# Layer 1's modulation groups 1 and 2 made as side steps of the latents' MLP in layer 0, loaded through GpSimd's queue

## The chip, the cores and the metric

The kernel runs on one core of a Trainium2 chip. The metric is the device time of one execution in microseconds; lower is better. A core has TensorE (PE, with its weight loads as PEld), VectorE (DVE), ScalarE (ACT), GpSimd (POOL) and SyncE (SP), which here only issues DMAs.

## The reference, cut to what matters

Two layers of a mixer network work on 256 latent tokens and 256 context tokens of width 1024, and a second network of two layers follows. Each of the first two layers begins with a modulation: one vector per stream goes through a matrix of 1024 x 6144, and its six parts shift, scale and gate the layer.

```
for i in range(DEPTH):
    m_l = (jax.nn.silu(c) @ mod_w + mod_b)[:, None, :]
    m_c = jax.nn.silu(c_ctx) @ mod_w + mod_b
    sh1_l, sc1_l, g1_l, sh2_l, sc2_l, g2_l = jnp.split(m_l, 6, axis=-1)
    ...
    p_lat = _ada(x, norm1, sh1_l, sc1_l) @ w_in
    p_ctx = _ada(ctx, norm1, sh1_c, sc1_c) @ w_in
    ... mixer (even: attention and rwkv; odd: ssd and gla) -> o_l, o_c
    x = x + g1_l * (o_l.astype(x.dtype) @ w_out)
    x = x + g2_l * _sq_relu_mlp(_ada(x, norm2, sh2_l, sc2_l), mlp_w1, mlp_w2)
```

The modulation depends on `c` and `c_ctx` alone, so it can be made at any time before its parts are read. Shift and scale 1 are read by layer 1's first norms, gate 1 by its output product, the rest by its MLP.

## The kernel before

All is float32. A product splits each operand into a rounded part and a remainder (`hi`, `lo`; ACT makes `hi` on L45, DVE `lo` on L46) and is made of three matmuls (`mm3`, L231 to L233). Weights come as tiles `w` of 128x1024 (512 KB), four buffers in the pool `wpool`, loaded by SP's queue in program order (`Stream.raw`, L32). One product tile of 128x256 with eight blocks of weights takes one `w` tile and 24 matmuls.

A modulation matrix is made in three groups of columns (`mod_steps`). A group has 16 units; a unit is one `w` tile of 512 KB and four narrow matmuls (128 rows, 32 columns, 256 wide; each stands in the trace as two instructions, L162) that add up in one PSUM bank. Two units are a step, with a `yield` behind it. Behind the last step ACT copies the bank (L166), PE transposes it four times (L169), and DVE adds the bias into `mT` (L171). With a `ring` the units are loaded into a ring of its own, four buffers, by the named engine; without one they go through SP's queue and the four buffers of `wpool`.

The latents' MLP of layer 0 (the call of `mlp` in `layer1`) has four parts of 16 product tiles each, 64 in all, eight of the first product and eight of the second. Its list `side` is advanced at n = 2 and 6 of each eight, so 16 times: two empty steps, the tables of the second network's rotation, the eight steps of layer 1's group 0 (ring of four buffers, GpSimd's queue, PSUM tag `po`), and the context's norm, whose first two tiles come together with the tail of group 0.

Then layer 1 norms the latents, makes the input product's first columns, and starts two mixers. `gla` (linear attention with gates) is a long chain of small DVE, ACT, POOL and PE work; its first half is written out ahead of the conv loop. The conv loop makes eight product tiles (512 wide, the last two 256), runs a five tap convolution over each (L860, L862) and a silu (L1223, L1225). Groups 1 and 2 of layer 1's modulation are written out behind the first of them, in one piece, through SP's queue and `wpool`, PSUM tag `mm` (two banks, which the conv products use too). Behind the loop come the second half of `gla`, eight products for `z` and `gs`, and the mixer `ssd`.

The order on each engine is not that of the program: a planner simulates the program with costs of its own and puts on each engine the ready instruction of highest priority, the priority being the order in which it was written out. On the chip each engine then takes its instructions strictly in that order, and each queue its DMAs. A side step is thus an instruction that the planner may take earlier, when it holds the engine for idle.

Of the kernel before, what the change touches and what calls it, by code (L numbers as in the profile page):

```python
# [76 lines left out]
class Kern:  # L77
# [720 lines left out]

        return h, sm, step

    def mlp(self, l, mp, x, w, sm, h=None, done=None, side=(), tags=("mm", "mm")):

        side = iter(side)
        nc, parts = self.nc, MLP_PARTS[l]
        g2 = self.ada(self.mT[l], self.V(f"norm2_{l}"), 3, mp, f"g2_{l}")
        with self.tc.high_priority():
            f = sm.rstd()
            early, h = h, []
            steps = self.norm_steps(mp, mp, x, f, w, g2, self.mT[l][:, 24:32, :], "h")
            if not early:  # L810
                h.extend(steps)
        NF = 7 if early else 0
        st = Stream(self, self.a[f"mlp{l}"])
        b0 = 0
        m = 32 // parts
        for i in range(parts):
            u = []
            for n in range(m):
                if i == 0 and n >= NF:
                    h.extend(steps)  # L820
                ps = self.gemm(st, b0, early if i == 0 and n < NF else h, tag=tags[n % 2])
                b0 += 8
                if n % 4 == 2:
                    next(side, None)
                r = mp.tile([P, 256], F32, tag="hf", name="relu", bufs=2)
                if i == 0 and n < NF:
                    b = mp.tile([P, 1], F32, tag="bias", name="bias", bufs=2)
                    nc.vector.tensor_copy(b, ps[:, 256:257])
                    nc.vector.tensor_tensor(r, ps[:, 0:256], f, op=ALU.mult)
                    nc.scalar.activation(r, r, AF.Relu, bias=b)  # L830
                else:
                    nc.scalar.activation(r, ps, AF.Relu)
                nc.scalar.activation(r, r, AF.Square)  # L833
                u.append(self.split(mp, r, 256, f"u{n}_"))
                if i == 0 and n < NF:
                    h.extend(itertools.islice(steps, 1))
            if i == 0:
                h.extend(steps)
            for n in range(8):
                ps = self.gemm(st, b0, u)  # L840
                b0 += m
                nc.vector.scalar_tensor_tensor(x[n], ps, self.mT[l][:, 40 + n, w : w + 1], x[n], op0=ALU.mult, op1=ALU.add)
                if done and i == parts - 1:
                    done(x[n])
                if n % 4 == 2:
                    next(side, None)
        for _ in side:
            pass
# [297 lines left out]
    def layer1(self, xc, xl, sm, hm, HL):  # L1146

        tc, nc, a = self.tc, self.nc, self.a
        L1, H, G = ExitStack(), ExitStack(), ExitStack()
        pool = lambda n, st=L1, side="left": st.enter_context(tc.tile_pool(name=n, bufs=1, side=side))  # L1150
        rp, kvp = pool("cossin", self.ctx), pool("kvp", self.ctx)
        pl, hl, hc = pool("l1"), pool("h1l"), pool("h1c", H)
# [6 lines left out]
        h = []  # L1159

        def norm(p, x, sm, w):
            g1 = self.ada(mT, self.V("norm1_1"), 0, pl, f"g1_1{w}")
            with ExitStack() as M:
                xp = pool("x1", M)
                h.append([])
                for i in self.norm_steps(xp, p, x, sm.rstd() if sm else self.rms(xp, x), w, g1, mT[:, 0:8, :], "h"):
                    h[-1].append(i)
                    yield

        with ExitStack() as M:  # L1170
            self.gap(M, 64)
            mp = pool("mlp", M, "right")
            sm, sm2 = Sum(self), sm

            def side():
                yield
                yield
                with ExitStack() as R:
                    rope.extend(self.rope2(pool("rope", R), rp))
                yield  # L1180
                yield from self.mod_steps(1, 0, mp, "po", (mp, 4, nc.gpsimd))
                for i, _ in enumerate(norm(hc, xc, None, 1)):
                    if i % 2:
                        yield

            rope = []
            self.mlp(0, mp, xl, 0, sm2, hm, sm.add, side(), ("mm", "po"))
        HL.close()
        lg = pool("lg", G)
        up = self.load("gk_up", lg)  # L1190
# [11 lines left out]
        for kk in range(8):  # L1202
            w = st.cols(40 * 128 + 512 * kk, 512)
# [13 lines left out]
        cp = pool("cv", C, "right")  # L1217
        cw, cb = [self.small(self.V(n), ALU.mult, 0.5, tag=n, pool=cp) for n in ("conv_w", "conv_b")]

        def silu(t, last):  # L1220

            u = cp.tile([P, 512], F32, tag="th", name="th")[:, : t.shape[-1]]
            i = nc.scalar.activation(u, t, AF.Tanh)  # L1223
            self.issue(i, last)
            nc.vector.scalar_tensor_tensor(t, u, 1.0, t, op0=ALU.add, op1=ALU.mult)  # L1225
            return i

        tanh, mods = [], (x for i in (1, 2) for x in self.mod_steps(1, i, cp, "mm"))
        for i in range(8):
            t = (xs + bm + cm)[i]  # L1230
            self.conv(cp, self.gemm(st, 72 + 8 * i, *(h if i < 6 else h[1:])), i, t, cw, cb)
            if i == 0:
                for _ in mods:
                    pass
            tanh.append(silu(t, last))
        for _ in mods:
            pass
        self.table(tanh)
        for _ in gla:
            pass  # L1240
# [22 lines left out]
        with ExitStack() as B:  # L1263
# [4 lines left out]
            h, sm, step = self.mlp_enter(1, pool("mh1", HL, "right"), 0)  # L1268
# [566 lines left out]
```

## Time and profile before

| what | us |
|---|---|
| median of 3 runs (lowest, highest) | 2023.52 (2015.88, 2032.34) |
| the profiled execution | 2024.35 |
| its span in the trace | 2022.6 |
| PE busy in the span | 1894.8 (94%) |
| DVE busy | 1420.9 (70%) |
| ACT busy | 1160.8 (57%) |
| POOL busy | 285.5 (14%) |

What lies around the span is 1.75 us. Matmuls are pipelined and their ends are modelled, so PE busy is not PE at its peak. Times of day in this text are us from the start of the span.

### The profile page before, as it was taken

What the parts mean: (1) busy time and instruction counts of PE and PEld (TensorE: products, weight loads), DVE (VectorE), ACT (ScalarE), POOL (GpSimd) and SP (SyncE); (2) the same over time, 40 slices, a digit from 0 to 9 for tenths busy, and PEclk for the clock granted to TensorE, in tenths of its full rate; (3) what the DMA queues carried; (4) which work ended last, traced back from release to release, by engine and by line L of the source; (5) the groups of instructions that cost most, each with busy time, mean ns of one, the idle gap of its engine ahead of it and who ended that gap; (6) DMA issues with size and microseconds to landing.
All of it is one profiled execution on the core that took longest, in us unless ns stands there. A gap on an engine that the chain in (4) does not pass through costs nothing.

```text
span 2022.6 us, 42324 instructions
## 1 busy us (share of the span) xinstructions
PE 1894.8 (94%) x16330; PEld 1709.2 (85%) x16330; DVE 1420.9 (70%) x2962; ACT 1160.8 (57%) x2527; POOL 285.5 (14%) x423
## 2 busy tenths in 40 slices
PE   5999989889999999999979999999999999989997
PEld 2986668669889998999638779999889999879997
DVE  3775966589767685576678978567777666677664
ACT  3654653465646676565545758476565555465553
POOL 1421110230100000001230210000012211002210
PEclk8999989899999999999979999999999999999999
DMA  8542530635116676755366435666325554324553
GB/s 304 165 137 76 171 126 22 199 95 166 43 35 189 188 238 203 244 176 167 120 222 189 143 105 175 186 187 189 124 84 168 188 188 146 103 86 157 187 187 116
DMA packets 91785, 313.26 MB, mean 155 GB/s; under 512 B 10304, under 2 KB 17728, under 8 KB 91584
## 3 DMA queue, kind: packets, MB, share of 16 engines
q1 hardware_dynamic: 81072, 291.55, 44.9%
q10 hardware_dynamic: 8208, 10.63, 1.7%
q0 software_dynamic: 2304, 8.39, 1.2%
q8 instruction: 128, 2.10, 0.4%
q14 instruction: 73, 0.60, 0.1%
HBM read 309.48 MB, written 1.05 MB: 154 GB/s over the span
## 4 chain that ended last, share of the span: by engine, by line
PE 73%; DVE 12%; ACT 5%; DMA 5%; issue 3%; POOL 2%; POOLq 0%; ACTq 0%; SPq 0%; DVEq 0%
PE mm L232 15%; PE mm L233 15%; PE mm L231 15%; PE po L232 3%; PE po L231 3%; PE po L233 3%; DMA w<-in_mod 2%; DVE lo L46 2%; DMA w<-in_w_in 2%; PE sc L540 1%; PE mm L162 1%; PE po L1395 1%; ACT hi L45 1%; DMA m<-in_memT 1%; PE po L1458 1%
## 5 line engine op out<-in xcount | busy, mean ns | idle before, releaser
L46 DVE TENSOR_TENSOR lo<-w,hi 128x512 fp32r<-128x512 f32 x948 | 654.6, 696 | 259.2 <-ACT hi L45 240.5
L45 ACT CAST hi<-w 128x512 fp32r<-128x512 f32 x948 | 577.4, 618 | 408.0 <-PE mm L232 308.3
L231 PE MATMUL mm<-u_h,hi 128*128 128x256 f32 x1120 | 314.3, 281 | 0.0
L233 PE MATMUL mm<-u_h,lo 128*128 128x256 f32 x1120 | 314.1, 281 | 0.0
L232 PE MATMUL mm<-u_l,hi 128*128 128x256 f32 x1120 | 313.3, 280 | 0.1
L231 PEld LDWEIGHTS mm<-u_h,hi 128*128 128x128 f32 x1120 | 210.5, 188 | 2.2 <-ACT hi L45 1.2
L232 PEld LDWEIGHTS mm<-u_l,hi 128*128 128x128 f32 x1120 | 210.9, 188 | 0.3 <-DVE u_l L225 0.3
L233 PEld LDWEIGHTS mm<-u_h,lo 128*128 128x128 f32 x1120 | 210.8, 188 | 0.1
L162 PE MATMUL mm<-w,cs 128*32 128x256 f32 x640 | 68.9, 452 | 30.8 <-DMA w<-in_mod 30.5
L1600 POOL TENSOR_TENSOR ut<-ut,gt 128x256 f32<-128x256 f32 x44 | 54.4, 1237 | 193.0 <-ACT hi L45 164.6
L162 PEld LDWEIGHTS mm<-w,cs 128*32 128x32 f32 x640 | 18.6, 118 | 59.4 <-DMA w<-in_mod 35.2
L225 DVE TENSOR_TENSOR u_l<-relu,u_h 128x256 fp32r<-128x256 f32 x96 | 40.8, 426 | 30.0 <-ACT u_h L224 29.8
L355 POOL TENSOR_SCALAR sht<-shf,mu 128x256 f32<-128x256 f32 x28 | 37.6, 1341 | 110.1 <-ACT shf L353 110.1
L224 ACT CAST u_h<-ut 128x256 fp32r<-128x256 f32 x44 | 17.9, 407 | 59.0 <-POOL ut L1600 59.0
L225 DVE TENSOR_TENSOR u_l<-ut,u_h 128x256 fp32r<-128x256 f32 x44 | 18.7, 425 | 45.0 <-ACT u_h L224 45.0
L264 POOL TENSOR_SCALAR hf<-hf,g,mT 128x256 f32<-128x256 f32 x24 | 18.7, 779 | 211.3 <-ACT h1h L263 111.8
L231 PE MATMUL mm<-h0h,hi 128*128 128x256 f32 x130 | 39.8, 308 | 7.4 <-ACT shf L353 3.6
L1552 POOL TENSOR_TENSOR xl<-xl,yy 128x256 f32<-128x256 f32 x16 | 14.2, 889 | 225.5 <-DVE yy L1551 225.5
L69 POOL TENSOR_TENSOR sq<-sq 128x256 f32<-128x256 f32 x24 | 20.7, 863 | 153.5 <-ACT sq L61 150.5
L233 PE MATMUL mm<-h0h,lo 128*128 128x256 f32 x130 | 38.4, 295 | 3.1 <-DVE lo L46 3.1
L833 ACT ACTIVATE relu<-relu 128x256 f32<-128x256 f32 x96 | 39.7, 417 | 2.4
L224 ACT CAST u_h<-relu 128x256 fp32r<-128x256 f32 x96 | 38.6, 405 | 2.3
(1126 smaller groups left out, 6096.6 us busy)
## 6 DMA issues: line engine op xcount, KB each, us to landing
w<-in_mlp SPq DMA_DIRECT2D x192, 512.0 KB, 4.1
w<-in_w_in SPq DMA_DIRECT2D x102, 512.0 KB, 4.1
w<-in_ffn_in SPq DMA_DIRECT2D x88, 512.0 KB, 4.1
w<-in_mod SPq DMA_DIRECT2D x80, 512.0 KB, 5.2
w<-in_ffn_out SPq DMA_DIRECT2D x44, 512.0 KB, 4.6
w<-in_w_out SPq DMA_DIRECT2D x40, 512.0 KB, 4.5
w<-in_mod POOLq DMA_DIRECT2D x16, 512.0 KB, 8.0
w<-in_memkv SPq DMA_DIRECT2D x8, 512.0 KB, 4.0
```

The costliest lines, as they stand in the source:

```text
L45: nc.scalar.copy(self.hi, w)
L46: nc.vector.tensor_tensor(self.lo, w, self.hi, op=ALU.subtract)
L69: self.eng.tensor_tensor(sq, sq, self.acc, op=ALU.add)
L162: nc.tensor.matmul(ps[32 * j : 32 * j + 32, o : o + 256], lhsT=self.cs[:, k, :], rhs=w[:, 256 * j : 256 * j + 256], start=(k == 0), stop=( ...
L224: nc.scalar.copy(hi, src)
L225: nc.vector.tensor_tensor(lo, src, hi, op=ALU.subtract)
L231: nc.tensor.matmul(out, lhsT=wh, rhs=xh, start=start, stop=False)
L232: nc.tensor.matmul(out, lhsT=wh, rhs=xl, start=False, stop=False)
L233: nc.tensor.matmul(out, lhsT=wl, rhs=xh, start=False, stop=stop)
L355: nc.gpsimd.tensor_scalar(t, f[:, 1:257], self.mu1[:, i : i + 1], None, op0=ALU.mult)
L833: nc.scalar.activation(r, r, AF.Square)
L1600: nc.gpsimd.tensor_tensor(w, w, t, op=ALU.mult)
```

## The change

The side list of the MLP is advanced at every second product tile (n = 1, 3, 5, 7 of each eight), so 32 times instead of 16. Behind the context's norm it has the steps of groups 1 and 2 of layer 1, through the same ring of four buffers on GpSimd's queue and the PSUM tag `po`; with the two tails these take just the 16 calls that were added. The conv loop loses them: their loads leave SP's queue and `wpool`, their matmuls leave the loop, and the tile `modsb` leaves its pool. The MLP of layer 1 and that of the context keep the old distance (the default of 4) and have no side list.

```
-    def mlp(self, l, mp, x, w, sm, h=None, done=None, side=(), tags=("mm", "mm")):
+    def mlp(self, l, mp, x, w, sm, h=None, done=None, side=(), tags=("mm", "mm"), every=4):
...
-                if n % 4 == 2:
+                if n % every == every // 2:
                     next(side, None)
...
-                if n % 4 == 2:
+                if n % every == every // 2:
                     next(side, None)
...
                 for i, _ in enumerate(norm(hc, xc, None, 1)):
                     if i % 2:
                         yield
+                for i in (1, 2):
+                    yield from self.mod_steps(1, i, mp, "po", (mp, 4, nc.gpsimd))
 
             rope = []
-            self.mlp(0, mp, xl, 0, sm2, hm, sm.add, side(), ("mm", "po"))
+            self.mlp(0, mp, xl, 0, sm2, hm, sm.add, side(), ("mm", "po"), 2)
...
-        tanh, mods = [], (x for i in (1, 2) for x in self.mod_steps(1, i, cp, "mm"))
+        tanh = []
         for i in range(8):
             t = (xs + bm + cm)[i]
             self.conv(cp, self.gemm(st, 72 + 8 * i, *(h if i < 6 else h[1:])), i, t, cw, cb)
-            if i == 0:
-                for _ in mods:
-                    pass
             tanh.append(silu(t, last))
-        for _ in mods:
-            pass
         self.table(tanh)
```

## Rows read from the trace of the kernel before

**Rows 1.** The page, part 4: the chain's share of the span, by engine.

```profile
PE 73%; DVE 12%; ACT 5%; DMA 5%; issue 3%; POOL 2%; POOLq 0%; ACTq 0%; SPq 0%; DVEq 0%
```

**Rows 2.** Instructions of L162 over the whole span: count, ns min/median/max, first and last.

```profile
L162 PE MATMUL mm<-w,cs x640: 378/403/637, 10.0 to 1071.0; 128*32 128x256 f32 x160
...
L162 PE MATMUL po<-w,cs x128: 378/379/404, 759.7 to 873.9; 128*32 128x256 f32 x128
```

**Rows 3.** Issues of SP's queue from 985 to 1080: start, us, what, count.

```profile
987.76 77.02 SPq L32 DMA_DIRECT2D w<-in_mod  x29
1064.89 15.08 SPq L32 DMA_DIRECT2D w<-in_w_in  x7
```

**Rows 4.** PE in order of time: the conv products' last and next matmul.

```profile
998.18 0.28 PE L233 MATMUL mm<-h7h,lo 128*128 128x256 f32 x1
...
1073.82 0.38 PE L231 MATMUL mm<-h0h,hi 128*128 128x256 f32 x1
```

**Rows 5.** The chain from 985 to 1135: shares by line, and its longest piece.

```profile
by line: PE mm L231 12.1%; PE mm L233 12.0%; PE mm L232 11.9%; PE mm L162 10.3%; DMA w<-in_mod 5.8%; issue 5.1%; PE po L1084 4.7%; PE po L1141 3.7%; DVE own L1094 3.1%; DVE mm L1090 2.5%; DVE gx L1064 2.2%; PE po L1142 2.1%; DVE cum L1046 1
...
1028.39 8.77 DMA w<-in_mod
```

**Rows 6.** Windows: length, PE, PEld, DVE, ACT, POOL busy, PEclk, DMA share, GB/s.

```profile
985.00:1135.00 150.00, 134.39 (x1377) 100.24 (x1376) 124.15 (x266) 92.39 (x223) 29.94 (x60) 0.92 0.59 188
985.00:1030.00 45.00, 38.27 (x480) 21.47 (x478) 39.10 (x76) 31.33 (x86) 21.48 (x36) 0.96 0.47 153
...
1090.00:1120.00 30.00, 29.91 (x246) 29.15 (x245) 28.92 (x51) 22.53 (x43) 0.53 (x8) 1.00 0.55 163
```

**Rows 7.** What DVE waited for from 985 to 1135: us, times, longest.

```profile
DVE lo L46 <- ACT hi L45: 5.2, 7, 1.3
DVE mm L1090 <- PE po L1087: 3.8, 3, 2.0
DVE dt L894 <- PE sc L892: 3.3, 1, 3.3
DVE mT L171 <- PE mm L169: 3.0, 1, 3.0
```

**Rows 8.** DVE in order of time: three product tiles of the MLP as they end.

```profile
823.28 0.48 DVE L842 SCALAR_TENSOR_TENSOR xl<-mm,mT,xl 128x256 f32<-128x256 f32 x1 [0.18 <-PE mm L233]
827.31 0.48 DVE L842 SCALAR_TENSOR_TENSOR xl<-mm,mT,xl 128x256 f32<-128x256 f32 x1 [0.18 <-PE mm L233]
830.13 0.48 DVE L842 SCALAR_TENSOR_TENSOR xl<-mm,mT,xl 128x256 f32<-128x256 f32 x1 [0.19 <-PE mm L233]
```

**Rows 9.** The chain through the MLP, 720 to 965: a stall, one step, one tail.

```profile
764.55 2.35 issue
766.92 5.11 DMA w<-in_mod
...
823.24 1.00 PE po L162 x16
...
885.78 0.44 PE po L169 x4
```

**Rows 10.** Windows in the MLP, columns as in rows 6.

```profile
823.00:873.00 50.00, 50.00 (x451) 47.13 (x449) 29.34 (x49) 28.15 (x56) 3.14 (x6) 1.00 0.71 233
849.00:859.00 10.00, 10.00 (x91) 9.82 (x84) 5.75 (x10) 7.14 (x17) 1.05 (x2) 1.00 0.82 270
...
773.00:778.00 5.00, 5.00 (x32) 5.00 (x31) 1.40 (x3) 1.24 (x2) 0.00 (x0) 0.66 0.91 362
```

**Rows 11.** DMA issues at 849, at 710 and from 840 to 880: KB, us to landing.

```profile
w<-in_mod POOLq DMA_DIRECT2D x2, 512.0 KB, 8.6
...
w<-in_mod POOLq DMA_DIRECT2D x4, 512.0 KB, 10.0
...
w<-in_mlp SPq DMA_DIRECT2D x13, 512.0 KB, 4.3
```

**Rows 12.** POOL in order of time: two loads of the ring.

```profile
849.15 1.05 POOL L32 DMA_DIRECT2D w<-in_mod  x2 [11.46 <-PE po L162]
```

## The prediction

> **What bounds the kernel now.** I read the page's chain first: PE has 73% of it [rows 1], so a stage that keeps PE full pays for each matmul added to it, and a stage where PE waits may lose matmuls for less than their length. The change takes from one kind of stage and gives to the other, so each must be read alone. The instructions of L162 say where the modulation is now [rows 2]: 128 under the tag `po`, in the MLP, are group 0 of layer 1, eight instructions to a unit; the two moved groups, 256 instructions, are among those under `mm`.
>
> The stage that loses them runs from 985 to 1135. SP's queue issues 29 of their loads in one run, and the next weights of the input product leave only at 1064.89 [rows 3]. So the conv products stop: the second one ends on PE at 998.18 and the third begins at 1073.82 [rows 4], while `gla` and the modulation share PE. The chain of these 150 us has 10.3% on L162 and 5.8% on waits for their loads, 15.5 and 8.7 us, with one wait of 8.77 us [rows 5]. Still PE is not the only busy engine: DVE has 124.15 of the 150 us [rows 6].
>
> The stage that gets them is the MLP, 735 to 935. From 823 to 873 PE is busy for all 50 us at the full granted clock, DVE for 29.34 [rows 10]. PE is the bound and nothing is idle there that a step could use.
>
> **The part that leaves.** 32 units at half of 1.00 us (two units take 1.00 us [rows 9]) are 16 us of PE, with two tails. If nothing else limited the stage, it would lose what the chain shows, 24.2 us: the upper bound, as the chain can't give more than it holds in this order. But the conv loop's work is not removed; it moves forward into the time that the modulation held. DVE's 124.15 us (less 0.8 of additions in the two tails, left out here) stay. So the question is how densely DVE can work. Where `gla` is its main work and gives it chains of short instructions, it was busy 39.10 of 45 us, 0.87; where conv and weight splits feed it, 28.92 of 30, 0.96 [rows 6]. At 0.87 the stage would take 142.9 us, a gain of 7; at 0.96 it is 128.8, a gain of 21. The new stage is both kinds mixed, with a filler for most gaps, so I take 0.92, near the middle: 134.9 us, **a gain of 15**. A second reading agrees: of DVE's 25.85 idle us, those put down to PE work that stood behind modulation loads are 3.8, 3.3 and 3.0, and 5.2 more are splits waiting for ACT as the conv loop refills [rows 7], together 15.3. PE holds 134.39 us there, some 118 without the moved work, so it comes behind DVE, if not by far. The granted clock of 0.92 [rows 6] may rise to 1.00 as PE is fuller; as DVE is next, I give that nothing.
>
> **The part that is added.** One step in the full MLP: the tiles that end at 823.28 and 827.31 are 4.03 us apart, the next pair, without a step, 2.82 [rows 8]. A step costs 1.21 us: 1.00 for 16 instructions [rows 9] and 0.21 of change over. The 16 steps of the two groups cost 19.4 us, their tails 0.44 each for the transposes [rows 9]: **20.2 us more**. The lower bound takes 1.00 for a step and is 16.9; none of it is hidden, since PE has no idle time. Doubling the calls moves group 0 and the context's norm forward, without adding to them. ACT's copy and DVE's additions of the tails lie beside PE.
>
> **The ring and the transfers.** With a step at every second tile, a period is 2 x 2.82 + 1.21 = 6.85 us, and in it two tiles of MLP weights and two units must arrive: 4 x 524288 bytes, 306 GB/s, for 16 periods, some 110 us. Before, the stretch with steps needed 233 GB/s at a DMA share of 0.71, in its fullest part 270 at 0.82, and PE never waited [rows 10]. The nearest row with both queues at work above that is a burst of 5 us at 362 [rows 10]: the rate can be had, for how long the trace doesn't show. The Trainium skill ("DMA: Bandwidth & Descriptors", section "Issuing engines are not separate DMA queues") speaks against the change: a DMA started by GpSimd runs on the same 16 DMA engines as SP's and interleaves with them, so another queue gives no transfers of its own, only issue time. The trace agrees so far that a unit through POOL lands later (8.6 us) than an MLP tile through SP (4.3) [rows 11]. By that rule the move would be worth its DMA share and no more, which is the first rival below.
>
> What must hold is the ring's turn. A slot is free when its step is done; POOL issues both loads in 1.05 us [rows 12]; the unit is needed two periods after the step that freed it began, 13.7 us. Less the step's 1.0 and the issue's 1.05, 11.7 us are left. Landing takes 8.6 us with two in flight and 10.0 with four [rows 11]. So it fits, with 2 to 3 us to spare. Bounds: nothing, or 16 periods stretched to the 270 GB/s that were shown for longer than a burst, 7.77 us each, 14.6 in all. As no wait is seen at 270 itself, I stay near the lower end: **2.5 us**. POOL's own queue gets 32 issues of 0.53 us; behind a load that waits for its slot stand at most norm tiles (L264), of which none falls into the 16 added calls. SP's queue loses the 32 loads.
>
> The stall at 764.55, 2.35 + 5.11 us [rows 9], is group 0's: the planner put its first units in a burst that emptied the ring, and PE stood until a load came that was issued too late. It may stay, go, or appear again; I let it stand as it is. `modsb` leaves the conv pool, so tiles that are allocated behind it move by 2 KB and may meet other former owners; nothing in the trace shows it, its cost is bounded by the longest single wait of DVE, 3.3 us [rows 7], either way, and I take nothing.
>
> **Sum**, against the profiled execution of 2024.35 us (1.75 us around its span; the median of 2023.52 is 0.04% lower, so no correction): 2024.35 + 20.2 + 2.5 - 15 = **2032 us**, 0.4% slower, within what can be told from no change. A measurement of this kernel tells some 1% (20 us) from nothing; its three runs spread over 16 us.
>
> **The rivals.** *The ring comes late (slower).* Decides from a landing time above 11.7 us. At 14 us a period becomes (14 + 2.05) / 2 = 8.0 us, 1.15 more in each of 16: 18.4 us in place of 2.5, so 2048. For it: the demand is above any stretch longer than a burst, and units already land in twice an MLP tile's time. Against: 362 GB/s for 5 us, no PE wait at 270. By the skill's rule above this is the outcome. Chance 0.17.
>
> *All of the chain comes back (gain).* DVE is packed as in rows 6's best stretch or better, the chain's 24.2 us go and no load is late: 2024.35 + 20.2 - 24.2 = 2020. For it: fillers of 0.7 us stand ready throughout. Against: `gla`'s chains kept DVE at 0.87 even where the modulation had hardly begun. Chance 0.18.
>
> *Bursts.* The planner does with each new group what it did at 764: four ready units at once, then PE stands 7.5 us, two times: 2032 + 15 = 2047. Against: in the full part of the MLP the planner has nobody idle to give a burst to. Chance 0.06.
>
> *It does not do what it says.* If the planner holds loads for late, the last steps slide behind the MLP, into 935 to 952, where the norm waits. They cost PE about the same there; the time is the forecast's. It and other shuffles of the planner have 0.02.
>
> **How the numbers follow.** The forecast, 0.57, has 2023 to 2040 as its own range (gain 10 to 21, loads 0 to 5). The range for 8 in 10 reaches halfway through the rivals: 2015 to 2050. Faster by over 1% (under 2004) would need the whole chain and the stall of 7.5 us besides, and more: 0.03. Slower by over 1% (above 2044) is the first and third rival without their lower parts: 0.20. The rest, 0.77, is within 1%.
>
> **What would show it.** Right: 256 more instructions of L162 under `po` between some 835 and 930, 16 groups of 16, product tiles 4.03 us apart at each; the MLP some 20 us longer; no `in_mod` waits in the conv loop; conv products running on from 998; DVE at about 0.92 until `z` and `gs` are done, some 135 us after the stage's start. Wrong: PE waits for `in_mod` inside the MLP, or landing times of POOL's units above 11.7 us (first rival); a stage of 126 us (second); gaps of 7 us at the start of a group (third); MLP tiles with late weights, which I hold for unlikely with SP's landing time of 4.3 us.

## The result, and the profile after

The changed kernel takes 2040.14 us (median of 14 runs, 2035.55 to 2048.85), the kernel before 2021.53 in the same comparison (14 runs): ratio **1.0096 [1.0078, 1.0114]**. A second comparison of the same two kernels gave 1.0069 [1.0045, 1.0093]. The two intervals overlap from 1.0078 to 1.0093, 16 to 19 us: slower, and by about as much as the forecast's bound of 1%. The forecast was 2032 us, 7.7 above the kernel before; the median lies at the upper end of the forecast's own range (2023 to 2040).

The page of the kernel after, the same parts as [rows 1] and the ones around it: busy time by engine, the granted clock in 40 slices, the queue of GpSimd's loads, the chain by engine.

```profile
PE 1902.3 (94%) x16330; PEld 1717.1 (84%) x16330; DVE 1417.5 (70%) x2962; ACT 1159.6 (57%) x2527; POOL 307.6 (15%) x455
...
PEclk8999989889999999999968999999999999999999
...
q0 software_dynamic: 6912, 25.17, 3.8%
...
PE 75%; DVE 12%; ACT 4%; DMA 4%; issue 3%; POOL 2%; POOLq 0%; ACTq 0%; DVEq 0%; SPq 0%
```

PE's busy time grows by 7.5 us and its share of the chain by 2 points. The clock's digits 6 and 8 stand in slices 21 and 22, which begin at 1017 us: the conv loop. Before, the same two digits were 7 and 9.

The instructions of L162, to be held against [rows 2]: the 256 have gone over from `mm` to `po`, and the last one is at 948.7, where the prediction had some 930.

```profile
L162 PE MATMUL mm<-w,cs x384: 379/403/637, 10.2 to 389.5; 128*32 128x256 f32 x192
...
L162 PE MATMUL po<-w,cs x384: 379/379/403, 759.0 to 948.7; 128*32 128x256 f32 x192
```

To see where the time went I cut the span at three instructions that stand in every kernel: the first sum of squares behind the MLP's entry (L65 under `sc`), the last copy of `v` (L1210 before, L1212 after), and the ssd's first score product (L987). The first and last start of each line are given; before first.

```profile
L65 PE MATMUL sc<-sq,c_cst x24: 377/379/484, 734.0 to 2009.7; 128*128 128x256 f32 x24
...
L1210 ACT COPY v<-po x2: 587/587/587, 984.5 to 985.9; 128x512 f32<-128x512 f32 x2
...
L987 PE MATMUL sc<-lt,c_cst x16: 592/593/697, 1154.1 to 1177.7; 128*128 128x512 f32 x16
```

The same three lines of the kernel after:

```profile
L65 PE MATMUL sc<-sq,c_cst x24: 377/378/484, 735.8 to 2020.3; 128*128 128x256 f32 x24
...
L1212 ACT COPY v<-po x2: 586/587/588, 1004.9 to 1006.3; 128x512 f32<-128x512 f32 x2
...
L987 PE MATMUL sc<-lt,c_cst x16: 592/593/1193, 1165.3 to 1191.3; 128*128 128x512 f32 x16
```

(The expectations call the second cut the end of the copies of `v`; the copy's start is meant.) From the first cut to the second ("MLP", with the norm and the small products behind it) it is 985.9 - 734.0 = 251.9 us before and 270.5 after: 18.6 lost. From the second to the third ("stage") 168.2 and 159.0: 9.2 won. From there to the end of the span 868.5 and 868.9. What lies ahead of the first cut is code that nothing here touches; it took 729.8 to 741.5 us in the fourteen profiles of this study, also between two profiles of one kernel. So kernels are compared by these parts below, and by ratios. A part is read from one execution, the profiled one; a ratio comes from all of them.

Two windows of the kernel after (columns as in [rows 6]): the full MLP with the new steps, and the prediction's own stretch of the stage, from the copies of `v` to `z` and `gs`.

```profile
842.00:950.00 108.00, 108.00 (x1013) 96.48 (x1012) 60.13 (x104) 59.56 (x119) 14.77 (x28) 1.00 0.90 295
1005.40:1146.00 140.60, 120.53 (x1110) 100.96 (x1109) 122.19 (x257) 89.40 (x221) 31.57 (x60) 0.81 0.26 81
```

In the MLP PE has no idle time and the full clock; 295 GB/s were carried for 108 us. The chain in order of time shows the steps 6.85 us apart (7.30 where the tail of group 1 stands between), each 1.00:

```profile
844.87 1.00 PE po L162 x16
...
851.72 1.00 PE po L162 x16
...
858.58 1.00 PE po L162 x16
```

In the stage DVE has 122.19 of 140.6 us, 0.87, at a mean clock of 0.81. In slices of 15 us:

```profile
1006.30:1021.30 15.00, 13.03 (x101) 9.24 (x102) 12.58 (x24) 12.28 (x26) 3.43 (x5) 1.00 0.22 72
1021.30:1036.30 15.00, 10.47 (x136) 7.55 (x136) 14.14 (x25) 11.44 (x33) 8.60 (x15) 0.89 0.01 2
1036.30:1051.30 15.00, 14.13 (x159) 9.65 (x157) 12.71 (x28) 8.21 (x28) 8.92 (x15) 0.50 0.12 37
1051.30:1066.30 15.00, 11.97 (x113) 8.62 (x110) 12.64 (x29) 8.56 (x23) 4.14 (x7) 0.50 0.00 1
1066.30:1081.30 15.00, 5.72 (x99) 4.38 (x101) 13.83 (x38) 5.72 (x19) 3.97 (x9) 0.50 0.00 0
1081.30:1096.30 15.00, 14.65 (x117) 12.66 (x111) 12.26 (x32) 4.18 (x16) 1.03 (x2) 0.79 0.34 99
```

The clock falls to 0.50, the lower of its two levels (1.2 GHz), and stays there for 45 us. Ahead of the fall PE had worked on `gla`'s short products and a few conv products, 10.47 of 15 us. PE in order of time shows it in single instructions, and what became of the conv products that [rows 4] had standing still:

```profile
1018.53 0.28 PE L233 MATMUL mm<-h7h,lo 128*128 128x256 f32 x1
1018.65 0.28 PE L231 MATMUL mm<-h0h,hi 128*128 128x256 f32 x1
...
1034.02 0.41 PE L232 MATMUL mm<-h0l,hi 128*128 128x256 f32 x1
...
1044.08 0.58 PE L233 MATMUL mm<-h4h,lo 128*128 128x256 f32 x1 [0.68 <-DVE lo L46]
...
1061.85 0.58 PE L233 MATMUL mm<-h0h,lo 128*128 128x256 f32 x1 [0.85 <-DVE lo L46]
```

The third product begins right behind the second, as forecast. The ones behind it come apart: from 1034 on they wait for `lo`, the weight splits that stand behind `gla`'s work in DVE's queue, and a matmul of 256 columns takes 0.41 in place of 0.28.

### The profile page after: what moved, and what is told of

Same layout as the page of the kernel before. It is cut to its first block, busy times and chain, and to the rows that moved or that the text cites. A ratio compares the mean times of both kernels' runs of the same rounds, so it can differ in the third digit from the quotient of the medians.

```text
span 2034.2 us, 42309 instructions
## 1 busy us (share of the span) xinstructions
PE 1902.3 (94%) x16330; PEld 1717.1 (84%) x16330; DVE 1417.5 (70%) x2962; ACT 1159.6 (57%) x2527; POOL 307.6 (15%) x455
## 4 chain that ended last, share of the span: by engine, by line
PE 75%; DVE 12%; ACT 4%; DMA 4%; issue 3%; POOL 2%; POOLq 0%; ACTq 0%; DVEq 0%; SPq 0%
PE mm L231 16%; PE mm L233 15%; PE mm L232 15%; PE po L232 3%; PE po L231 3%; PE po L233 3%; DVE lo L46 2%; DMA w<-in_w_in 2%; PE sc L540 1%; PE po L162 1%; PE po L1392 1%; DMA w<-in_mod 1%; ACT hi L45 1%; PE po L1455 1%; DVE yy L1548 1%
## 5 line engine op out<-in xcount | busy, mean ns | idle before, releaser
L32 POOL DMA_DIRECT2D w<-in_mod x48 | 25.7, 539 | 233.4 <-PE po L162 129.4
L162 PE MATMUL mm<-w,cs 128*32 128x256 f32 x384 | 41.1, 481 | 20.4 <-DMA w<-in_mod 20.0
L162 PEld LDWEIGHTS mm<-w,cs 128*32 128x32 f32 x384 | 11.9, 124 | 40.2 <-DMA w<-in_mod 20.5
L69 POOL TENSOR_TENSOR sq<-sq 128x256 f32<-128x256 f32 x24 | 20.7, 863 | 153.5 <-ACT sq L61 150.5
L231 PEld LDWEIGHTS mm<-h0h,hi 128*128 128x128 f32 x130 | 24.9, 193 | 20.8 <-ACT shf L353 6.2
```

Of the source, the lines that this page charges most:

```text
L32: eng.dma_start(w, self.dram[u // 2][:, (u % 2) * 1024 : (u % 2) * 1024 + 1024])
L69: self.eng.tensor_tensor(sq, sq, self.acc, op=ALU.add)
L162: nc.tensor.matmul(ps[32 * j : 32 * j + 32, o : o + 256], lhsT=self.cs[:, k, :], rhs=w[:, 256 * j : 256 * j + 256], start=(k == 0), stop=( ...
L231: nc.tensor.matmul(out, lhsT=wh, rhs=xh, start=start, stop=False)
```

## The experiments

**My theory** after the result: the MLP's part costs what it was priced at, and the gain is smaller than 15 us because the groups' products, which lose little in the stage, had kept TensorE's clock up beside `gla`. **Rivals**: VectorE's queue alone bounds the stage, and the clock is of no account; or the order, conv behind `gla`, is at fault. Each ratio is to the kernel before, run beside it. The parts of each (us; the second number of a pair is another profile of the same kernel):

| kernel | ratio to before | MLP | stage | loads, products in the stage |
|---|---|---|---|---|
| before | 1 | 251.9, 250.3 | 168.2, 168.8 | 32, 256 |
| after | 1.0096, 1.0069 | 270.5, 270.4 | 159.0, 158.4 | 0, 0 |
| without the groups | 0.9985 | 250.3 | 157.7 | 0, 0 |
| made in both places | 1.0123 | 270.5 | 166.4 | 32, 256 |
| products without loads | 0.9994 | 251.8 | 153.5 | 0, 256 |
| loads without products | 0.9991 | 251.8 | 160.6 | 32, 0 |
| after, with resident products | 1.0074 | 273.3 | 154.3 | 0, 256 |
| spread over the loop | 1.0128 | 252.0 | 187.9 | 32, 256 |
| one group moved | 0.9983, 1.0006 | 260.7, 261.6 | 152.2, 156.5 | 16, 128 |
| after, two loads in the MLP | 1.0058 | 270.9 | 160.3 | 0, 0 |

**Without the groups.** The kernel before with the conv loop of the kernel after, and nothing in the MLP; the two groups are left out.

```diff
-        tanh, mods = [], (x for i in (1, 2) for x in self.mod_steps(1, i, cp, "mm"))
+        tanh = []
...
-            if i == 0:
-                for _ in mods:
-                    pass
...
-        for _ in mods:
-            pass
```

> The kernel before without layer 1's modulation groups 1 and 2: neither their loads, nor their matmuls, nor their tails, in either place; the columns that they would fill are set to zero. This is the gain of the removal alone. Theory A (VectorE bounds the conv and gla stage at the density that gla gives it, 0.87): the stage falls from 150 to some 142 us, so 8 us under the kernel before, about 2013. Theory B (the chain's 24 us come back, and the changed kernel lost them to something that is in the MLP or in its steps): about 1997. If TensorE's fallen clock costs the stage, the trace shows PEclk at 0.5 to 0.6 in it, as in the changed kernel, and the gain is 8 or less for that reason.

Measured: 2018.37 us (10 runs), ratio 0.9985 [0.9967, 1.0002]. Neither theory had this time (2013 and 1997). The removal alone is worth some 3 us by the ratio (0 to 7 by its interval) and 10.5 in the stage of its profile; 15 is out of reach either way. The clock falls as in the kernel after:

```profile
1019.30:1034.30 15.00, 14.13 (x168) 9.67 (x167) 12.90 (x28) 8.20 (x28) 8.86 (x15) 0.59 0.12 38
1034.30:1049.30 15.00, 10.60 (x111) 7.69 (x111) 13.76 (x32) 9.20 (x24) 4.27 (x8) 0.64 0.01 1
1049.30:1064.30 15.00, 5.72 (x101) 4.65 (x101) 14.23 (x42) 6.27 (x19) 3.53 (x9) 0.50 0.01 2
```

**Made in both places.** The kernel after with the old conv loop put back, so that only the MLP's part of the change is left.

```diff
-        tanh = []
+        tanh, mods = [], (x for i in (1, 2) for x in self.mod_steps(1, i, cp, "mm"))
...
```

> The changed kernel with the two groups made a second time at their old place behind the first conv product, through SP's queue. This is the cost of the MLP's part alone, against the kernel before: my sum has 20.2 us for the steps and tails and nothing measured for late loads, so about 2041; if the steps cost more than the tile spacing shows, above 2045; if part of the steps lies in idle time, under 2035.

Measured: 2044.38 us (4 runs), ratio 1.0123 [1.0087, 1.016], 25 us; in its profile the MLP is 18.6 longer and the stage 166.4. By the ratios, the two halves of the change (this one and the one above) add up to 1.0108, near the 1.0096 measured for the whole. In the profiles the MLP's part is 18.6 to 20.2 us; by the ratio it is 18 to 32.

**Products without loads.** No group is made, but the same 256 products run in the conv loop on the latents, which are resident:

```diff
...
+                for n in range(2):
+                    ps = self.psum("mm")
+                    for u in range(16):
+                        for j in range(4):
+                            nc.tensor.matmul(ps[32 * j : 32 * j + 32, u // 8 * 256 : u // 8 * 256 + 256], lhsT=self.cs[:, u % 8, :], rhs=xl[(u + j) % 8], start=(u % 8 == 0), stop=(u % 8 == 7))
...
```

> As the run without the two groups, but the 256 instructions of their matmuls stand in the conv loop at the old place, with a resident tile in place of the loaded weights; their loads, tails and results are left out. Loads block (the conv loop's weights wait in SP's queue behind them): the time is that of the run without the groups, within 4 us. Matmuls cost: it lies 8 us or more above that run, near the kernel before. Clock: the matmuls keep TensorE at its higher level while gla runs, and the time is under that of the run without the groups, by up to 10 us.

Measured: 2016.67 us (10 runs, 2006.35 to 2030.3), ratio 0.9994 [0.9966, 1.0023]. The ratio can't tell it from the run without the products, nor from the kernel before. In its profile the stage takes 153.5 us, 4.2 less than with no products at all; but the profiled execution was the fastest of the ten (2006.35) and had the highest mean clock of them (0.979). Its two cuts and the slices of the stage:

```profile
L1211 ACT COPY v<-po x2: 586/586/587, 981.0 to 982.4; 128x512 f32<-128x512 f32 x2
...
L988 PE MATMUL sc<-lt,c_cst x16: 592/594/1061, 1135.9 to 1161.2; 128*128 128x512 f32 x16
...
1012.40:1027.40 15.00, 13.18 (x256) 7.43 (x251) 14.83 (x30) 9.67 (x30) 8.75 (x15) 1.00 0.13 38
1027.40:1042.40 15.00, 12.74 (x188) 9.31 (x185) 13.51 (x36) 7.88 (x25) 4.43 (x8) 1.00 0.01 2
1042.40:1057.40 15.00, 11.46 (x150) 9.54 (x150) 13.85 (x39) 8.70 (x22) 4.85 (x6) 0.89 0.13 37
```

256 products more, and the clock is at 1.00 where it was at 0.50 to 0.64.

**Spread over the loop.** The kernel before with three steps of the groups behind each conv product, in place of all behind the first.

```diff
-            if i == 0:
-                for _ in mods:
-                    pass
+            for _ in itertools.islice(mods, 3):
+                pass
```

> The kernel before with the two groups spread over the conv loop, three steps behind each product, in place of all behind the first; nothing is moved to the MLP. If the block of loads in SP's queue is what costs, conv products run on between them, and 8 to 15 us go: 2006 to 2013. If VectorE's density bounds the stage anyway, some 5 to 8 us: 2013 to 2017. If the matmuls and load waits stall gla as before, no change: 2021.

Measured: 2046.46 us (4 runs), ratio 1.0128 [1.0084, 1.0173], 26 us slower, where all three expectations had the same time or less. The stage grows to 187.9. The steps reach into the time behind `gla`, where loads of the groups and of `w_in` come at 270 GB/s and more while DVE is busy for less than half of the time:

```profile
1096.50:1111.50 15.00, 12.36 (x100) 9.22 (x100) 5.64 (x9) 4.70 (x8) 0.13 (x2) 0.77 0.75 270
1111.50:1126.50 15.00, 9.74 (x68) 8.02 (x72) 7.26 (x11) 4.05 (x7) 0.14 (x2) 0.77 0.84 278
```

So the place that the kernel before gave to the groups, all of them behind the first product, is better in this loop than a spread: there they end at 1071 [rows 2], and the third conv product follows at 1073.82 [rows 4].

**The kernel before once more**, for a second profile.

> The kernel before, unchanged, for a second profile and a null comparison. All theories: ratio 1.000 within 0.003; in the profile 251.9 us within 1 from the first sum of squares of the MLP (L65) to the end of the copies of v, and 168 us within 4 from there to the first score product of the ssd (L987). What lies ahead of the MLP (734.0 us in the profile before, 730.6 to 741.5 in the six profiles so far) is code that no edit here touches; if it differs by some us between profiles of one kernel, that is the spread of the medians.

Measured: ratio 1.0013 [0.9994, 1.0031]; MLP 250.3, stage 168.8, 737.1 us ahead of the MLP. The stage's 168 is no accident of one profile, and the 3 us by which the time ahead of the MLP differs are one source of the spread of the times.

**After, with resident products.** The block of products from above, put into the conv loop of the kernel after.

> The kernel after, with 256 matrix products more of the groups' form on resident data in the conv loop, where the groups were made before; they write a bank that nobody reads, and load nothing. Clock theory (the groups' products had kept TensorE's clock at its upper level behind gla): the granted clock stays at 1.00 through the stage, which falls from 159.0 to 154 us, and the time is about 5 us under the kernel after: 2035 us, ratio 1.007. Rival (VectorE's queue alone bounds the stage, the clock is of no account there): 256 products more cost nothing or up to 10 us, 2040 to 2050 us, ratio 1.0095 to 1.014.

Measured: 2034.89 us (4 runs), ratio 1.0074 [1.0044, 1.0104], where the clock theory had 2035 and 1.007. In its profile, again the fastest execution (2028.26), the stage is 154.3, at full clock until 1063; its MLP is 2.8 longer than in the kernel after, where the stall at the front, 5.47 us there, is 7.23 here.

```profile
1033.50:1048.50 15.00, 13.17 (x256) 7.49 (x256) 14.83 (x31) 9.64 (x29) 8.76 (x15) 1.00 0.13 38
1048.50:1063.50 15.00, 12.73 (x187) 9.24 (x184) 13.51 (x36) 7.95 (x25) 4.41 (x8) 1.00 0.01 2
1063.50:1078.50 15.00, 12.14 (x151) 10.30 (x149) 13.85 (x39) 8.69 (x22) 4.84 (x6) 0.77 0.13 36
```

The ratio lies between the two of the kernel after (1.0069 and 1.0096), so the times don't show the 5 us, and they don't exclude the rival's "nothing". What speaks for the clock theory are the stages, 157.7 against 153.5 and 159.0 and 158.4 against 154.3, each time with the fastest execution on the shorter side.

**Conv first.** The kernel after, with the conv products' priority raised in the order of every engine.

```diff
-            self.conv(cp, self.gemm(st, 72 + 8 * i, *(h if i < 6 else h[1:])), i, t, cw, cb)
+            with self.tc.high_priority():
+                self.conv(cp, self.gemm(st, 72 + 8 * i, *(h if i < 6 else h[1:])), i, t, cw, cb)
```

> The kernel after, with the eight conv products, their weight splits and taps given priority over gla's work in the order of every engine. Rival (the splits of conv's weights stand behind gla's work in VectorE's queue, and that is why the products did not run on): the stage is 5 to 10 us shorter than 159.0, 2030 to 2035 us, ratio 1.0045 to 1.007. Clock theory: products run earlier and keep the clock up while gla waits, so 4 us come back as in the run with resident products, but no more. Density theory (VectorE's 140 us of work and the gaps that gla's chain leaves in it): the stage stays within 3 us of 159, since gla now ends later by what conv ends earlier; 2037 to 2043 us.

Measured: 2047.77 us (4 runs), ratio 1.0133 [1.011, 1.0155]: slower than the kernel after (its first interval is just touched), which no theory had. The conv products now begin ahead of the last copy of `v` (at 1043.9 in this kernel), so the stage's cut has no meaning; from the MLP to the ssd it is 431.8 us against 429.5. `gla` then runs with less beside it, at clocks of 0.61 to 0.84. So conv ahead of `gla` is no remedy; a smaller raise, of the splits alone, was not tried.

**Loads without products.** The kernel before with the 32 loads in their place, but neither products nor tails.

```diff
-        tanh, mods = [], (x for i in (1, 2) for x in self.mod_steps(1, i, cp, "mm"))
+        tanh, ms = [], Stream(self, a["mod1"])
...
-                for _ in mods:
-                    pass
+                for u in range(32):
+                    ms.raw(16 + u)
...
```

> The kernel before, with the 32 loads of the two groups left in the conv loop, through the same ring and queue, but none of their 256 products and no tails (modulation groups 1 and 2 of layer 1 are left at zero). If the cost of the groups there was TensorE waiting in its order for the loads: the stage takes what it took with neither loads nor products, 157.7 us, 2018 us. If the cost was that the weights of the conv products stand behind 32 loads in SyncE's queue and in the ring: the stage stays at 164 to 170 us, 2021 to 2026 us, and the third conv product runs no earlier than before, about 88 us after the stage begins.

Measured: 2019.14 us (10 runs), ratio 0.9991 [0.997, 1.0012]; stage 160.6, nearer to the first of the two expectations (157.7) than to the second (164 to 170).

```profile
992.20:1007.20 15.00, 13.54 (x125) 9.06 (x125) 12.51 (x24) 11.62 (x25) 5.49 (x8) 1.00 0.90 323
1007.20:1022.20 15.00, 7.22 (x87) 4.86 (x81) 13.47 (x27) 9.25 (x30) 6.75 (x12) 0.51 0.92 341
1022.20:1037.20 15.00, 12.65 (x168) 8.19 (x164) 14.17 (x30) 10.19 (x32) 8.23 (x17) 0.50 0.94 342
```

With nobody to wait for, the 32 loads leave SP's queue in 52 us from 976.8 on, at 323 to 342 GB/s in these slices, and cost 3 us of the stage (160.6 against 157.7). In the kernel before, 29 of the same loads took 77 us [rows 3]: the slots of `wpool` come free only as PE gets to the products. Its slices in the middle of this time, to be held against those above:

```profile
1030.90:1045.90 15.00, 11.53 (x146) 5.54 (x146) 10.91 (x35) 6.39 (x19) 3.05 (x6) 0.66 0.68 241
1045.90:1060.90 15.00, 10.35 (x139) 5.59 (x132) 12.18 (x36) 4.50 (x17) 2.55 (x5) 0.76 0.74 249
```

TensorE's clock dips here too, to 0.66 and 0.76, in the stretch of the long wait for `in_mod` [rows 5], but for a shorter time. The third conv product begins at 1047.73 here, 55 us into the stage, about where the kernel with products and no loads has it (54 us); at clocks of 0.50 and 0.51, and beside the loads, this order brings no gain.

With this the four corners are there, in us of the stage:

| | 256 products | none |
|---|---|---|
| 32 loads | 168.2, 168.8 | 160.6 |
| none | 153.5, 154.3 | 157.7, 159.0, 158.4 |

Loads cost 3 without products and 15 with them; products cost 8 with loads, and -4 to -5 without. By these profiles, what the groups cost at their old place is PE waiting, in its order, for a load, less what the products give back. (154.3, 159.0 and 158.4 are from kernels with the MLP of the kernel after.) The times show much less: the ratios of the four corners lie between 0.9985 and 1, and none of their intervals leaves 1 out. The two profiles of before (2024.35 and 2023.62) lie above most medians of their kernel, 153.5 and 154.3 come from the fastest executions of theirs, and two profiles of one kernel can differ by 4.3 us in the stage (one group moved, below). So the 8 and the 15 stand in profiles alone, and the 3 and the 4 to 5 are no larger than that spread.

**The kernel after once more.**

> The kernel after, unchanged, for a second profile. The first one gave 270.5 us from the MLP's first sum of squares (L65) to the end of the copies of v and 159.0 us from there to the ssd's first score product (L987), against 251.9 and 168.2 to 168.8 us of before: +18.6 and -9.5. All theories: the same two lengths within 3 us, with a granted clock of 0.50 to 0.60 behind the stage's first 30 us; median 2036 to 2042 us, ratio 1.0075 to 1.0115.

Measured: 2036.56 us (9 runs), ratio 1.0069 [1.0045, 1.0093], MLP 270.4, stage 158.4, with clocks of 0.50 to 0.59 between 1036 and 1081. Ratio and median are at the lower edge of what was expected, the lengths and clocks in it.

**One group moved.** Group 1 beside the MLP, group 2 in the conv loop.

```diff
-                for i in (1, 2):
-                    yield from self.mod_steps(1, i, mp, "po", (mp, 4, nc.gpsimd))
+                yield from self.mod_steps(1, 1, mp, "po", (mp, 4, nc.gpsimd))
...
-        tanh = []
+        tanh, mods = [], self.mod_steps(1, 2, cp, "mm")
...
```

> Only one of the two groups moves: group 1 is made beside the MLP as in the kernel after, group 2 in the conv loop as before. MLP: 8 steps of 1.21 us and one tail, +10 us (252 to 262 us). In the stage 16 loads and 128 products are left. Clock theory: 16 loads at the 340 GB/s that the run with loads alone showed are down within 25 us, TensorE hardly waits for them, and the products keep the clock up in part: the stage takes 153 to 157 us, 12 to 15 less than before, and the whole is 2 to 5 us under before: 2016 to 2019 us, ratio 0.998 to 0.999. Rival (loads and products cost in proportion): half of each, +9.3 and -4.7, 2025 to 2030 us, ratio 1.0025 to 1.005.

Measured: 2021.64 us (10 runs), ratio 0.9983 [0.9963, 1.0004]. MLP 260.7, stage 152.2: half of the loads cost the stage nothing that can be seen, and half of the products hold the clock at 1.00 from 1031 to 1061:

```profile
1031.00:1046.00 15.00, 13.23 (x209) 6.92 (x208) 14.00 (x29) 10.77 (x33) 9.48 (x17) 1.00 0.63 200
1046.00:1061.00 15.00, 11.65 (x167) 9.04 (x168) 14.97 (x43) 10.45 (x28) 3.60 (x7) 1.00 0.43 150
```

As the only version that might beat both kernels it was measured once more:

> The kernel with one group moved, unchanged, in more rounds: does it beat the kernel before? By its first profile (MLP +8.8 us, stage 152.2 in place of 168.5) it is 7 us better behind the MLP's start, 2014 to 2017 us, ratio 0.9965 to 0.998; the first comparison gave 0.9983 [0.9963, 1.0004]. If that profile was a lucky one: ratio 0.999 to 1.001, and a stage of 155 us or more.

Measured: 2023.92 us (12 runs), ratio 1.0006 [0.9988, 1.0024]; its second profile has a stage of 156.5, at clocks of 0.76 to 0.90 up to 1077. So the first profile was the better one, and the kernel is as fast as the one before: it beats the kernel after, not before. Proportional cost (1.0025 to 1.005) lies outside both intervals, of the second one by a hair.

The two profiles are of one program, with every matmul and every DVE instruction in the same order, and so they show what the clock does by itself. The first slice of the stage, a conv product in it, and ACT's copy of the next product of `gla`, from the first profile:

```profile
1001.00:1016.00 15.00, 13.66 (x126) 9.02 (x126) 12.51 (x23) 11.62 (x25) 5.50 (x8) 1.00 0.11 36
...
1006.66 0.28 PE L231 MATMUL mm<-h7h,hi 128*128 128x256 f32 x1
...
1013.36 0.27 ACT L1113 COPY kt<-sc 128x128 f32<-128x128 f32 x1 [0.69 <-PE sc L1111]
```

The same from the second profile, with the wait of DVE behind that copy:

```profile
991.40:1006.40 15.00, 15.00 (x82) 10.11 (x83) 11.57 (x20) 9.76 (x20) 3.58 (x5) 0.66 0.12 36
...
998.80 0.41 PE L231 MATMUL mm<-h7h,hi 128*128 128x256 f32 x1
...
1007.27 0.27 ACT L1113 COPY kt<-sc 128x128 f32<-128x128 f32 x1 [4.22 <-PE sc L1111]
...
1007.88 0.29 DVE L1071 TENSOR_TENSOR kl<-k,gx 128x128 f32<-128x128 f32 x1 [2.44 <-ACT gx L1067]
```

At a clock of 0.66 in place of 1.00 PE gets through 82 matmuls in place of 126, ACT waits 4.22 us for it in place of 0.69, and DVE then stands for 2.44 us. That is more than half of the 4.3 us by which this stage is longer.

**Two loads in the MLP.** The kernel after, with one load for each group in place of 16.

```diff
-            w = st.raw(16 * g + u, ring)
+            if not (once and u):
+                w = st.raw(16 * g + u, ring)
...
```

> The kernel after, with all products of the two groups beside the MLP but one load for each group in place of 16 (groups 1 and 2 of layer 1 are made from the wrong weights). What the prediction put down to late loads (2.5 us) goes away if it was there: 2037 to 2038 us. If the ring of four on GpSimd's queue kept ahead all along, as the trace of the kernel after looks: no change within 1.5 us, and 268 to 271 us from the MLP's first sum of squares to the end of the copies of v. If the 265 to 310 GB/s of the MLP slowed the MLP's own weights, 5 us or more come back: 2035 us or less.

Measured: 2035.27 us (10 runs), ratio 1.0058 [1.0036, 1.008]; MLP 270.9 against 270.5. The loads cost the MLP nothing. The time is 1.3 us under that of the kernel after measured beside it (2036.56), which is the "no change within 1.5 us" of the expectation; the ratio's interval overlaps both of the kernel after, and neither the MLP nor the stage of its profile (160.3) is shorter.

## Why the prediction came out as it did

**The steps.** 16 steps of 1.21 and two tails, 20.2 us: the steps stand 6.85 us apart as worked out, and the MLP is 270.5 - 251.9 = 18.6 us longer in one pair of profiles, 270.4 - 250.3 = 20.1 in the other. (The ratio of the groups made in both places says 25, 18 to 32.)

**The ring.** 2.5 us for late loads; measured is nothing. PE has no wait for `in_mod` in the added steps, GpSimd's 28 loads from 842 on land in 7.0 to 10.8 us, median 8.3, under the 11.7 from which the first rival decides, and 30 loads less change the MLP by 0.4 us. The sharing is there: the MLP's own weights land 7.1 us after their issue in place of 4.3 [rows 11]. The Trainium skill's rule ("DMA: Bandwidth & Descriptors", section "Issuing engines are not separate DMA queues"), that DMAs started by different engines interleave on the same 16 DMA engines, agrees with that row. It cost no time here, as both streams were issued early enough; the late ring that the prediction drew from it did not come.

**The stall at the front** stayed, at 772.33 for 5.47 us, as assumed. No burst at a new group: the third rival is out.

**The gain, the term that was mis-sized.** The prediction took 15 us, from a DVE density of 0.92 between the bounds 0.87 and 0.96. Measured are 9.2 and, between the second profiles, 10.4 us by the cuts; the prediction's own stretch shows DVE at 122.19 of 140.6, the lower bound of 0.87. The step that failed is "with a filler for most gaps, so I take 0.92". The filler that was to make the stage dense, conv products, ran out of split weights at 1034. The second reading, 15.3 us of DVE's 25.85 idle us to go, failed with it: 18.4 are left. The remark that the clock "may rise to 1.00 as PE is fuller" had the sign wrong: it fell, to 0.50 for 45 us. The prediction gave the clock nothing, so no number of its sum hung on that, but the fall is the likely reason why the stage stayed at its lower bound.

For it speak two pairs of kernels that differ in such products alone (without the groups and products without loads; after and after with resident products). They show the clock, 0.50 to 0.64 for 45 us without, 1.00 with until 60 us into the stage, and they show the stage 4 to 5 us shorter with more work in it, at a density of 0.92 and 0.91 over the same stretch (124.71 of 136.1 us and 124.36 of 136.9). So 0.92 was right for a stage that keeps its filler, as far as two profiles show it, each of its kernel's fastest execution; the times show no gain of these products. That the clock is the cause is not proved by the pairs: the planner, given the products, also puts the third conv product later (1057.76 us in the kernel after with them, 1018.65 without), so that `gla` has fewer splits beside it on DVE. The run with conv first, where more of conv stands ahead of `gla`, is slower, which fits either reading. Two places tell clock and order apart in part: with loads alone the third product is as late as with the products, the clock low and the stage 160.6 (though the loads may have their share in that); and the two profiles of one group moved, one program in one order, differ by 4.3 us with the clock. So a lower clock does lengthen this stage by some us; how much of the 4 to 5 in the two pairs is the clock's stays open. The Trainium skill says of TensorE ("TensorE: Matmul & The Clock Gate", section "What's actually happening") that "the default state is throttled, and activity releases the throttle". The levels, 0.50 and 1.00, and the pairs with and without products agree; a busy PE alone does not show it, as PE was busy for 14.13 of 15 us at 0.50 from 1036.30 on.

**The sum.** 18.6 - 9.2 is 9.4 us in one pair of profiles; over both pairs, with what lies ahead and behind, the profiled executions are 2036.6 and 2024.0 in the mean: 12.6 apart. The ratios say 14 and 19. Some 2 to 6 us are thus in no profile. Part of them may be the spread of single executions: before was profiled at 2024.35 and 2023.62, while its medians in the five comparisons lie between 2020.75 and 2025.98. The rest stays open; a hint is that the clock over the whole span, which each run reports, reached 0.980 in the fastest runs of before (2009 us) and 0.969 at most in 23 runs of the kernel after, and that the medians of all kernels without products in the stage lie at 0.960 to 0.965, of those with products behind one another there at 0.969 to 0.973. That is argued, not shown.

**Luck.** The sum was 7.7 us and the ratios say 14 and 19, so it was about half of what came. The time fell inside the range because the range, 2015 to 2050, allowed for rivals that did not come; and the 2.5 us for late loads that were not late made up for part of the gain that was missing.

## What to carry to other kernels

Work that a profile shows on the chain may still be nearly free: before moving it, look at what its neighbours would do without it: at the clock, and at the order that the planner makes of what is left, as well as at the next-late engine. Price a step at its new place, on an engine that is full, at its whole length: in the profiles that was right to 2 us, and no gain of loads off a queue made up for it. A stage in one profile is one execution: see whether the times of all of them show its gain, and where among them the profiled one lies. Where work waits for loads, moving half of it may take the wait and leave the filler, though here that only came out even.

## What was not expected of the hardware

TensorE had more to do and the stage of the profile got shorter: with 256 products more, 16 us of it by the price of a step [rows 9], it took 154 us in place of 159. And the DMA engines carried two streams from two queues at 295 GB/s for 108 us with every weight in time, where the MLP of before showed 270 at most over more than a burst [rows 10]; in the conv loop with loads alone they reached 342.
